# Holding back the splits of the down weights from the eighth instead of the sixteenth step of the last gate-and-up chunk

## The chip, the cores and the metric

The kernel runs on one core of one Trainium2 chip. The metric is the device time of one execution in microseconds; the median over the runs shown is compared. A core has five engines with an instruction queue each, which work in the order of the program: TensorE (PE, with its weight loads PEld), VectorE (DVE), ScalarE (ACT), GpSimd (POOL) and SyncE (SP), which here only issues loads and stores. Queues wait for each other through semaphores.

## The reference

One decoder layer on 256 tokens of width 1024, in float32: a mixer (causal pooling beside block attention), a cross-attention into 256 memory tokens, and a SwiGLU feed-forward network of width 2816. Each is followed by a residual sum, scaled by 2^0.25, and a layer norm. The change lies in the last part:

```
h = layer_norm(DEEPNORM_ALPHA * h + swiglu(h, w_gate, w_up, w_down), ln3_g, ln3_b)

def swiglu(h, w_gate, w_up, w_down):
    return (silu(h @ w_gate) * (h @ w_up)) @ w_down
```

## The kernel before

**Float32 by parts.** A float32 operand is split into a rounded high part and the low rest; a product is then three matmuls, high by high, high by low and low by high (`three`, lines 386 to 388; in gate and up the first two are one matmul of 512 columns, line 401, and the third is line 407). The activations are split once. Every weight tile (128 x 1024 numbers, 512 KB) is loaded into a raw tile, cast to its high part by ScalarE, and the low part is subtracted by VectorE (line 173).

**The stream of weights.** All weight tiles are numbered in the order of their use in one `Stream`, `ws`. There are seven raw tiles (`RAW_BUFS`), and eight buffers for split tiles and one more late in the kernel, so `ahead` is nine. `prepare` emits the split of the next tiles, and afterwards `fetch_ahead` emits loads until seven raw tiles are out and not yet split. `next`, called when a tile has been used, and `get`, called when one is wanted, prepare at most one further tile, up to nine past those used, unless `ws.held` is set; then `next` does nothing and `get` prepares only the tile that it needs itself. Where a split is emitted sets its place in the queues of ScalarE and VectorE.

**Gate and up.** The 2816 columns are worked in 11 chunks of 256 (`NFC`). A chunk has four weight tiles, w99 to w102 in the last one, and four PSUM banks, two for gate and two for up. `proj_both` yields 16 steps per chunk. In the last three chunks they go in groups of four: two steps with high parts, two with low parts; each fourth step has used up one weight tile and calls `next`. After the chunk, `Gated.add` sums the banks into SBUF (ScalarE copies at line 987, VectorE adds at line 988). `multiply` (lines 992, 993) and `split` (lines 453, 454, and 1004 to 1007 where sums are needed) follow inside the next chunk, after its second and its fourth step, and for the last chunk inside the down projection.

**Down.** Each chunk of 256 gated columns meets two tiles of w_down. Eight of the eleven chunks are multiplied as 2 x 2 blocks with seven products instead of eight, summed into eight PSUM banks m0 to m7. Four of them (`seven`, w103 to w114) build the sums of weights on VectorE and ScalarE in `prepare_pair` (lines 134 to 147): a pair is loaded as two tiles and prepared in three steps, which give three split tiles, the third, w105 for the first pair, from sums alone. The other four (`summed`, w115 to w128) load sums that transfers have made before. The last three chunks (`LAST`, w129 to w134) are multiplied plainly in `pieces`, which reads their tiles four times in all for different output columns. m1, m2, m3 and m5 take the banks of one pool, m7, m6, m4 and m0, in this order, those of the other, in which the last chunk of gate and up was summed. The first two splits of a pair are thus those around the change: w109 is the first and w110 the second of the third pair.

Behind the down products VectorE makes eight sums of m tiles and the residual (lines 1129 to 1145), adds what `pieces` yields (line 1132), takes the statistics (line 741), and the last norm follows. The end of the second half of the tokens goes through two float32 matmul pairs (lines 1180 and 1181), the second with a diagonal of the norm's scale that ScalarE makes (line 1178).

The lines around the change, with the steps counted:

```
run(gu, 2)                     # steps 1 and 2
if left: left.multiply()
run(gu, 2)                     # steps 3 and 4
if left: left.split()
if c == NFC - 1:
    run(gu, 2 * KD - 5)        # 11 more, to step 15
    ws.held = True
run(gu)                        # what is left
left = Gated(c, pss)
left.add()
# behind the loop:
ws.held = False
ws.next()
```

Of the kernel before, what the change touches and what calls it, by code (L numbers as in the profile page):

```python
# [18 lines left out]
KD = D // P  # L19
# [31 lines left out]
class Stream:  # L51
# [125 lines left out]
    def next(self):  # L177

        if not self.held:
            self.prepare(min(self.used + self.ahead, len(self.tiles) + 1))  # L180
# [27 lines left out]
def decoder_layer(  # L208
# [145 lines left out]
    def add_quarters():  # L354
        def add(dst, src):
            nc.gpsimd.dma_start(dst, src, accum_op=OP.add, max_dma_last_dim=8192)

        add(sum_z, w_sum[:, 2:4])
        add(sum_w, sum_z[:, 1:2].to_broadcast(list(sum_w.shape)))
        add(sum_w[:, 0], w_sum[:, 1])  # L360
# [32 lines left out]
    def proj_both(pss, numbers, yT, group=KD):  # L393

        for k0 in range(0, KD, group):
            for k in range(k0, k0 + group):
                hi, _ = ws.get(numbers, k)
                for b, ps in enumerate(pss):  # L400
                    nc.tensor.matmul(ps, hi[:, b * P:(b + 1) * P], yT.both(k), start=k == 0, stop=False,  # L401
                                     skip_group_check=True)
                yield
            for k in range(k0, k0 + group):
                _, lo = ws.parts_of(numbers, k)
                for b, ps in enumerate(pss):
                    nc.tensor.matmul(ps[:, S:], lo[:, b * P:(b + 1) * P], yT.pair(k)[0], start=False,  # L407
                                     stop=k == KD - 1, skip_group_check=True)
                ws.done(numbers, k)
                if ws.pace == 1:  # L410
                    ws.next()
                yield
# [31 lines left out]
    def run(gen, n=None):  # L444

        while n is None or n > 0:
            if next(gen, gen) is gen:
                return False
            n = None if n is None else n - 1
        return True  # L450
# [516 lines left out]
    def gated_t():  # L967
        pt = bank("pgt").rearrange("p (f t) -> p f t", f=2)
        for t in range(T):
            for f in range(2):  # L970
                nc.tensor.transpose(pt[:, f, t * P:(t + 1) * P], sg0[:, t, f * P:(f + 1) * P], ident)
        gated_parts(0)
        split(gT[0][0], gT[0][1], pt.rearrange("p f (t s) -> p (f t) s", t=T))
# [47 lines left out]
    for c in range(1, NFC):  # L1021
        pss = [(accbank if c % 2 else bank)("pg") for _ in range(4)]
        if c == 3:
            ws.widen(late)
            add_quarters()
        gu = proj_both(pss, c_gu[c], h2T, KD if c < NFC - 3 else 2)
        run(gu, 2)
        if left:
            left.multiply()
        run(gu, 2)  # L1030
        if left:
            left.split()
        else:
            run(gu, 4)
            gated_t()
        if c == NFC - 1:
            run(gu, 2 * KD - 5)
            ws.held = True
        run(gu)
        left = Gated(c, pss)  # L1040
        left.add()
# [199 lines left out]
```

## Time and profile before

| | |
|---|---|
| median of 3 runs | 382.67 us (382.51 to 382.80) |
| the profiled execution | 382.99 us |
| its span, first to last instruction | 381.2 us |
| mean granted TensorE clock | 0.988 |
| TensorE busy | 370.6 us, 97% of the span |
| VectorE, ScalarE busy | 303.7 us, 207.5 us |

All times within the kernel are microseconds from the start of the span of the profiled execution. A row of a timeline reads: start, duration, engine, line and operation, output and inputs, count, and in brackets the idle time before it and what ended that. A row of waits reads: who, at which line, waited for whom; microseconds in total, how often, the longest. A row of windows reads: the stretch, its length, busy time of TensorE, its weight loads, VectorE, ScalarE and GpSimd (with counts), the granted TensorE clock, the share of the DMA engines that was busy, and GB/s. Durations overlap a little with the next instruction, so a distance between two starts (a pitch) is shorter than a duration.

### The profile page before, as it was taken

The page shows a single profiled execution, that of the slowest core. Times are in us where ns is not written, and L with a number is a line of the kernel's source. Part 1 is how long each engine was busy: PE and PEld are TensorE (multiplying, and loading weights), DVE is VectorE, ACT ScalarE, POOL GpSimd, SP SyncE. Part 2 cuts the span into 40 slices and gives each one's busy share as a digit, 9 for nine tenths or more (in the row PEclk, how much of TensorE's full clock was granted, in tenths as well). Part 3 has the DMA queues.
Part 4 walks back from the last instruction along what each step waited for, and adds up shares of the span by engine and source line. Part 5 has one row for each costly group of instructions (what it writes and reads, how often), then busy time and mean ns, then how long its engine had stood idle before and what let it go on. Part 6 is the DMA issues. An engine that isn't in the chain of part 4 may idle for free.

```text
span 381.2 us, 5607 instructions
## 1 busy us (share of the span) xinstructions
PE 370.6 (97%) x2058; PEld 318.7 (84%) x2058; DVE 303.7 (80%) x490; ACT 207.5 (54%) x331; POOL 22.8 (6%) x30
## 2 busy tenths in 40 slices
PE   9999999999999999999999999999999995999994
PEld 8997878788888898988888888888898884888883
DVE  6868899965699758865887858888888899986974
ACT  5756677643164736544165666655675556766410
POOL 1000034300110000000111000000000000000021
PEclk9999999999999999999999999999999996999998
DMA  7996675578309953877179999766554134499202
GB/s 263 415 415 259 222 276 160 179 235 288 133 16 342 353 172 112 301 268 265 50 138 331 258 350 322 310 222 220 193 198 163 57 110 166 130 357 412 96 0 110
DMA packets 24268, 84.51 MB, mean 222 GB/s; under 512 B 2481, under 2 KB 3249, under 8 KB 23217
## 3 DMA queue, kind: packets, MB, share of 16 engines
q1 hardware_dynamic: 23120, 78.46, 56.7%
q0 software_dynamic: 688, 5.24, 6.7%
q10 hardware_dynamic: 432, 0.46, 0.3%
q8 instruction: 16, 0.26, 0.3%
q14 instruction: 12, 0.09, 0.1%
HBM read 83.10 MB, written 10.49 MB: 246 GB/s over the span
## 4 chain that ended last, share of the span: by engine, by line
PE 89%; DVE 6%; issue 2%; ACT 1%; DMA 1%; POOLq 0%; ACTq 0%; DVEq 0%
PE pg L401 15%; PE pg L407 8%; PE pqk L507 6%; PE m L386 5%; PE m L387 5%; PE m L388 5%; PE acc L386 4%; PE acc L387 4%; PE acc L388 4%; PE pxq L401 4%; PE pxk L401 4%; PE pxq L407 2%; PE pu L401 2%; PE pxk L407 2%; PE xv L386 2%; PE xv L388 2%
## 5 line engine op out<-in xcount | busy, mean ns | idle before, releaser
L453 ACT CAST g<-sg 128x512 fp32r<-128x512 f32 x16 | 9.9, 619 | 21.0 <-DVE sg L1007 15.1
L749 POOL TENSOR_TENSOR rs<-rs,mhalf 128x1 f32<-128x1 f32 x6 | 5.0, 832 | 264.0 <-DVE rs L748 264.0
L454 DVE TENSOR_TENSOR g<-sg,g 128x512 fp32r<-128x512 f32 x16 | 11.1, 692 | 9.6 <-ACT g L453 9.6
L988 DVE TENSOR_TENSOR sg<-pg,sg 128x256 f32<-128x256 f32 x40 | 14.1, 416 | 0.0
L992 ACT ACTIVATE sg<-sg 128x512 f32<-128x512 f32 x10 | 6.3, 632 | 14.3 <-DVE sg L988 14.3
L987 ACT COPY sg<-pg 128x256 f32<-128x256 f32 x40 | 11.8, 377 | 0.0
L544 ACT ACTIVATE xpr<-xs,mx 128x256 f32<-128x256 f32 x8 | 3.7, 470 | 14.3 <-DVE mx L555 14.3
L544 ACT ACTIVATE pr<-pr,mx 128x128 f32<-128x128 f32 (+1 forms) x16 | 7.1, 445 | 7.6 <-DVE mx L575 7.6
L453 ACT CAST h2T<-tp 128x512 fp32r<-128x512 f32 x4 | 2.3, 586 | 12.9 <-PE tp L464 12.9
L754 DVE SCALAR_TENSOR_TENSOR r<-r,mv,gb 128x512 f32<-128x512 f32 (+2 forms) x12 | 8.3, 723 | 0.0
L741 DVE BATCH_NORM_STATS2 st<-r 128x6 f32<-128x512 f32 (+1 forms) x12 | 8.0, 670 | 0.3
L993 DVE TENSOR_TENSOR sg<-sg 128x512 f32<-128x512 f32 x10 | 6.9, 692 | 0.8
L620 POOL TENSOR_TENSOR win<-upad 128x542 f32<-128x542 f32 x2 | 4.0, 2000 | 57.0 <-DVE upad L651 57.0
L549 DVE RECIPROCAL sm<-sm 128x2 f32<-128x2 f32 x12 | 2.0, 166 | 6.0 <-ACT xpr L544 4.5
L859 PE MATMUL xs<-xkTh,xq 128*128 128x256 f32 x32 | 6.4, 282 | 0.0
L453 ACT CAST h1T<-tp 128x512 fp32r<-128x512 f32 x4 | 2.4, 588 | 7.1 <-PE tp L464 7.1
L759 DVE SCALAR_TENSOR_TENSOR h<-r,rs,gb 128x512 f32<-128x512 f32 x8 | 5.7, 747 | 0.1
L620 POOL TENSOR_TENSOR win<-win 128x269 f32<-128x269 f32 (+3 forms) x4 | 5.8, 1444 | 0.2
L659 ACT CAST xkTh<-pxk 128x256 fp32r<-128x256 f32 x8 | 2.6, 377 | 5.5 <-PE pxk L407 5.5
L661 DVE TENSOR_TENSOR xkl<-pxk,xkTh 128x256 f32<-128x256 f32 x8 | 3.0, 415 | 3.1 <-ACT xkTh L659 3.1
L859 PEld LDWEIGHTS xs<-xkTh,xq 128*128 128x128 f32 x32 | 5.2, 190 | 0.2
L171 ACT CAST w39h<-w39r 128x1024 fp32r<-128x1024 f32 x1 | 1.0, 1049 | 7.8 <-PE acc L388 7.8
(1148 smaller groups left out, 1295.1 us busy)
## 6 DMA issues: line engine op xcount, KB each, us to landing
sum_z<-in_w_sum SPq DMA_DIRECT2D x1, 2048.0 KB, 10.4
sum_w<-in_w_sum SPq DMA_DIRECT2D x1, 2048.0 KB, 10.4
sum_z<-in_w_sum POOLq DMA_DIRECT2D x1, 2048.0 KB, 13.9
sum_w<-sum_z POOLq DMA_DIRECT2D x1, 2048.0 KB, 17.9
gb<-in_ln_g SPq DMA_DIRECT2D x3, 512.0 KB, 6.6
gb<-in_ln_b SPq DMA_DIRECT2D x3, 512.0 KB, 8.9
wr<-in_w_qkv SPq DMA_DIRECT2D x5, 256.0 KB, 4.5
mr<-in_mem_t SPq DMA_DIRECT2D x1, 1024.0 KB, 11.1
```

What stands on the lines that cost most here:

```text
L386: nc.tensor.matmul(ps, wa, ya, start=start, stop=False, skip_group_check=part)
L387: nc.tensor.matmul(ps, wa, yb, start=False, stop=False, skip_group_check=part)
L388: nc.tensor.matmul(ps, wb, ya, start=False, stop=stop, skip_group_check=part)
L401: nc.tensor.matmul(ps, hi[:, b * P:(b + 1) * P], yT.both(k), start=k == 0, stop=False, skip_group_check=True)
L407: nc.tensor.matmul(ps[:, S:], lo[:, b * P:(b + 1) * P], yT.pair(k)[0], start=False, stop=k == KD - 1, skip_group_check=True)
L453: nc.scalar.copy(h, ps)
L454: nc.vector.tensor_sub(l, ps, r32(h))
L507: nc.tensor.matmul(qk[i][:, f, :], w[:, c * P:(c + 1) * P], y, start=k == 0 and f == 0 and w is hi and y is x_hi, stop=k == KD - 1 and w i ...
L544: nc.scalar.activation(dst[:, j, :], src[:, j, :], AF.Exp, bias=mx[:, j:j + 1], scale=sign, accum_out=sm[:, j:j + 1])
L859: nc.tensor.matmul(ps[:, t, :], q[:, kk, t * P:(t + 1) * P], k[:, 2 * h + kk], start=n == 0, stop=q is q_lo and kk == 1, skip_group_check= ...
L987: nc.scalar.copy(y[:, f, :], ps[:, S:])
L988: nc.vector.tensor_add(y[:, f, :], ps[:, :S], y[:, f, :])
```

## The change

In the last chunk (c = 10) the hold is set after 3 more steps instead of 11, so after 7 of the 16 steps instead of 15. The preparation that steps 8 and 12 would emit is then left out there, as that of step 16 was already. The hold ends where it did, behind `left.add()`; the tiles are prepared from there on, one at each call of `next`.

```
         if c == NFC - 1:
-            run(gu, 2 * KD - 5)
+            run(gu, 3)
             ws.held = True
         run(gu)
         left = Gated(c, pss)
```

More of the change, by code (lines that the diff above doesn't have):

```diff
@@ L1036, in decoder_layer @@
         if c == NFC - 1:
-            run(gu, 2 * KD - 5)
+            run(gu, 3)
             ws.held = True
```

## The prediction

> **What bounds the kernel now.** I read the page first, then TensorE's waits, then the timeline of each engine from 310 us to the end, then VectorE's and the loads' rows for the down projection. The page says that TensorE is the bound almost everywhere, with one hole near the end.
>
> ```profile
> PE 370.6 (97%) x2058; PEld 318.7 (84%) x2058; DVE 303.7 (80%) x490; ACT 207.5 (54%) x331; POOL 22.8 (6%) x30
> PE   9999999999999999999999999999999995999994
> PEclk9999999999999999999999999999999996999998
> ```
>
> The 5 of the busy tenths and the 6 of the clock stand in slice 34 (each slice is 9.53 us, so about 314.5 to 324). The waits of TensorE name it, and a timeline of TensorE shows its size:
>
> ```profile
> PE m L386 <- DVE sg L988: 4.1, 1, 4.1
> 314.93 0.39 PE L388 MATMUL m<-w104h,g 128*128 128x512 f32 x1
> 319.38 0.80 PE L386 MATMUL m<-w104h,g 128*128 128x512 f32 x1 [4.07 <-DVE sg L988]
> 319.98 0.63 PE L387 MATMUL m<-w104l,g 128*128 128x512 f32 x1
> 328.70 0.39 PE L386 MATMUL m<-w109c,g 128*128 128x512 f32 x1
> 333.46 0.39 PE L386 MATMUL m<-w112c,g 128*128 128x512 f32 x1
> 317.00:318.00 1.00, 0.00 (x0) 0.00 (x0) 1.00 (x3) 0.22 (x2) 0.00 (x0) 0.81 0.00 0
> ```
>
> The fifth product of the down projection writes m7, whose PSUM bank is the first of the four in which the last chunk of gate and up was summed. That bank is free only when VectorE's first add (line 988) has read it. VectorE is busy the whole time; this is what it does meanwhile:
>
> ```profile
> 313.63 0.69 DVE L136 TENSOR_TENSOR w111r<-w109r 128x512 f32<-128x512 f32 x1
> 317.17 0.69 DVE L143 TENSOR_TENSOR w109r<-w110r,w109r 128x512 f32<-128x512 f32 x1
> 317.78 1.22 DVE L144 TENSOR_TENSOR w110l<-w111r,w110h 128x1024 fp32r<-128x1024 f32 x1
> 318.91 1.41 DVE L988 TENSOR_TENSOR sg<-pg,sg 128x256 f32<-128x256 f32 x4
> 320.24 1.22 DVE L147 TENSOR_TENSOR w111l<-w109r,w111h 128x1024 fp32r<-128x1024 f32 x1
> 321.37 0.69 DVE L993 TENSOR_TENSOR sg<-sg 128x512 f32<-128x512 f32 x1
> 322.74 0.69 DVE L454 TENSOR_TENSOR go<-sg,go 128x512 fp32r<-128x512 f32 x1 [0.69 <-ACT go L453]
> 323.35 0.69 DVE L136 TENSOR_TENSOR w114r<-w112r 128x512 f32<-128x512 f32 x1
> 326.90 0.68 DVE L143 TENSOR_TENSOR w112r<-w113r,w112r 128x512 f32<-128x512 f32 x1
> 327.50 1.22 DVE L144 TENSOR_TENSOR w113l<-w114r,w113h 128x1024 fp32r<-128x1024 f32 x1
> ```
>
> From 313.63 to 318.91 it splits w109 and w110, which TensorE reads only at 328.70 and later, while the adds that TensorE needs wait behind them in VectorE's order.
>
> **What the change moves.** In the last chunk the two splits that were emitted at its 8th and 12th step, w109 and w110, are held, so they come after the adds. Moved are seven instructions of VectorE (lines 136 to 140, 143, 144: 318.91 - 313.63 = 5.28 us) and three casts of ScalarE. These two calls of `prepare` issue no loads: with three pairs or their parts unsplit, `fetch_ahead` already has seven raw tiles out at w115, and it goes on only when w111 is split. The order of SP's loads is thus unchanged; POOL issues nothing here. Nothing is added or removed.
>
> **Term 1, TensorE at the seam.** VectorE comes to the adds at 313.63; TensorE has then finished the gate and up sums (its first eleven products of down are issued by 314.93), and ScalarE, without the three casts, is free for its copies. The first add takes 1.41/4, about 0.4 us: m7 is free at 314.05. TensorE would want it one pitch after its row at 314.93; 21 matmuls from 328.70 to 333.46 give a pitch of 0.227, so at 315.16. The wait is gone: 319.38 - 315.16 = 4.22 us. With it goes the half clock that the hole leaves behind (0.63 us for a matmul against 0.39): from 319.38 to 328.70 there are 30 matmuls in 9.32 us, and at the full pitch they take 6.80, so another 2.52. From w109 on TensorE could be 6.74 us earlier.
>
> **Term 2, the splits that come later.** After the adds the program's order on VectorE is w109, multiply (993), split of the gated tile (454), w110, w111, then w112. The same instructions as before lie between 313.63 and w112's first, so it starts at 323.35 again, plus one bubble: w111's cast on ScalarE waits for line 143 and VectorE then has only line 144 to fill with.
>
> ```profile
> 317.95 1.05 ACT L146 CAST w111h<-w109r 128x1024 fp32r<-128x1024 f32 x1 [0.78 <-DVE w109r L143]
> 335.73 0.39 PE L387 MATMUL m<-w113l,g 128*128 128x512 f32 x1
> ```
>
> The cast starts 0.78 us after line 143 does and takes 1.05; VectorE is free 0.61 + 1.13 after it; with a hand-over the bubble is 0.12. So w112 and all behind it come 0.12 later than before, while TensorE reads them 6.74 earlier. w109 (ready at 313.63 + 1.33 for the adds + 3.54 + the tail of its last instruction, 318.6) is wanted at 321.96. The tightest is w113's low part: ready at 327.50 + 1.22 + 0.12 = 328.84, wanted at 335.73 - 6.74 = 328.99. That cover is 0.15 us thick; if it is gone TensorE waits by what VectorE is late, and by term 3 up to 1 us of that costs nothing. The lead falls from nine tiles to seven, as `next` prepares one per tile used.
>
> **Term 3, the loads.** This is where the gain ends. The last tiles are bound by transfers:
>
> ```profile
> SPq L103 <- DVE w112r L143: 8.2, 1, 8.2
> 327.65 0.38 SPq L103 DMA_DIRECT2D w119r<-in_w_sum  x1
> 323.00:328.00 5.00, 5.00 (x20) 4.07 (x19) 5.00 (x8) 2.54 (x4) 0.00 (x0) 0.85 0.03 11
> 335.00:355.00 20.00, 20.00 (x90) 16.53 (x90) 15.26 (x13) 13.51 (x13) 0.00 (x0) 1.00 1.02 391
> 349.01 1.05 ACT L171 CAST w129h<-w129r 128x1024 fp32r<-128x1024 f32 x1 [1.44 <-DMA w129r<-in_w_down]
> 351.52 1.05 ACT L171 CAST w130h<-w130r 128x1024 fp32r<-128x1024 f32 x1 [1.46 <-DMA w130r<-in_w_down]
> 356.61 1.05 ACT L171 CAST w134h<-w134r 128x1024 fp32r<-128x1024 f32 x1 [0.20 <-DMA w134r<-in_w_down]
> 357.49 0.39 PE L387 MATMUL m<-w129l,go 128*128 128x512 f32 x1
> 358.85 0.39 PE L387 MATMUL m<-w130l,go 128*128 128x512 f32 x1
> ```
>
> SP waits 8.2 us for line 143 of w112 before it issues w119; the engines of the DMA idle (a share of 0.03 from 323 to 328), and from 335 to 355 they are full (1.02). So the stream of w119 to w134 starts when w112's line 143 ends and then runs at the rate of the transfers. Line 143 stays at 326.90 plus 0.12, so w134 lands where it did, plus 0.12. (w117 and w118, released by w109's line 143 and w110's 144, go out 3.3 us later, since 317.17 becomes about 320.5; they fall into the idle stretch.) TensorE, early by 6.74, wants w129's low part at 350.75 and w130's at 352.11 or later. Cast and subtraction end 1.09 + 1.23 us after a cast starts (as at 356.61 and 357.70, next fence), so they are ready at 351.45 and 353.96: TensorE waits 0.7, then about 1.2 more, and is early by 358.85 - 353.96 = 4.9 us from there on.
>
> **Term 4, VectorE's tail.** Behind w134's subtraction VectorE has eight sums of 0.6 us, then norm 3.
>
> ```profile
> 357.70 1.22 DVE L173 TENSOR_TENSOR w134l<-w134r,w134h 128x1024 fp32r<-128x1024 f32 x1
> 358.84 0.68 DVE L1129 SCALAR_TENSOR_TENSOR r<-h,m 128x512 f32<-128x512 f32 x1
> 364.94 1.37 DVE L1132 TENSOR_TENSOR r<-m,r 128x512 f32<-128x512 f32 x2 [1.22 <-PE m L388]
> 369.70 0.69 DVE L1132 TENSOR_TENSOR r<-m,r 128x512 f32<-128x512 f32 x1 [0.24 <-PE m L388]
> 371.85 0.42 DVE L1132 TENSOR_TENSOR r<-m,r 128x256 f32<-128x256 f32 x1 [0.73 <-PE m L388]
> 374.23 0.43 DVE L741 BATCH_NORM_STATS2 st<-acc 128x6 f32<-128x256 f32 x1 [1.49 <-PE acc L388]
> ```
>
> VectorE's waits for TensorE from here to the end are 1.22 + 0.24 + 0.73 + 1.49 = 3.68 us. With TensorE early by 4.9 all of them go; overlap with the next instruction (0.08 at each of the four places, 0.69 of duration against a pitch of 0.61) gives back another 0.3. VectorE then carries the end by itself. The later chain (mean, power on POOL, ScalarE's diagonal, two matmuls, copy, store) hangs on the last statistics and moves with them.
>
> **The sum.** 3.68 + 0.32 - 0.12 = 3.9 us. Against its own time, 382.99 for a span of 381.2, the profiled execution would be 379.1; the median shown, 382.67, lies 0.3 below that execution, which makes 378.8. The bounds: all of TensorE's 6.74 if nothing behind holds it back (375.9), and from the other side the whole 5.28 us of moved work landing on the release of w119 (3.9 - 5.3 = -1.4, so 384.1). I take the value near the first end, since VectorE's rows show no place where the moved work meets a wait.
>
> **Rivals.** *The half clock at the end.* TensorE would finish its last products and the first of its two final pairs 4.9 us earlier, but the last pair waits for the diagonal, only 3.9 earlier.
>
> ```profile
> 374.03 0.81 PE L1180 MATMUL end<-gb,ident 128*128 128x384 f32 x2
> 376.31 0.91 PE L1181 MATMUL end<-r,diag 128*128 128x384 f32 x2 [1.46 <-ACT diag L1178]
> 314.20:317.60 3.40, 1.12 (x5) 0.57 (x4) 3.40 (x6) 2.14 (x5) 0.00 (x0) 1.00 0.47 154
> ```
>
> The idle time of 1.46 becomes about 2.4. At the seam the clock fell 2.3 us after TensorE stopped (0.81 in the second from 317 means full speed until 317.62), at the end of a stretch in which it was still busy for 1.12 of 3.40 us. If it falls so again, the last pair takes 0.91 x 0.63/0.39 or more, so 0.6 to 0.9 longer, on the path: 379.6. [...]
>
> *The loads are not the bound.* If w119's stream came earlier with TensorE, up to 6.7 us would be gained: 376.0. Against it stand the full transfers from 335 to 355 and casts that wait for them to the end.
>
> *Slower: the release of w119 slips.* The held splits keep the raw tiles of w109 to w111 longer. If VectorE came to w112's line 143 not 0.12 but the whole 5.28 us later, because it had to wait after the adds for what the moved splits used to cover, the stream of loads and the end would move with it: 384.0. It decides from a slip of 4.0 us on, as the end depends on it one to one. For it: the stream has no slack. Against: only the waits of 0.69 and 0.12 stand in VectorE's new order.
>
> *Nothing much happens.* Another wait at the seam takes the place of this one (ScalarE's copies, or the down tiles starving TensorE from w112 on): 382.6. Against: m7's first reader is the only wait of TensorE there, and a starved TensorE costs nothing for its first microsecond.
>
> **How the numbers follow.** Forecast 0.60 (its own range 378.0 to 379.3), half clock 0.20, loads not the bound 0.07, slower 0.08, nothing much 0.05. About 0.2% is what a measurement of this kernel tells from no change. The range of 377.2 to 380.3 leaves out the three small cases, 0.2 in all. Faster: 0.60 + 0.20 + 0.07 and half of the last, 0.89; same 0.03; slower 0.08.
>
> **What would show it.** Right: no wait of TensorE at line 386 for line 988, no half clock near 320; line 988 at about 313.6, ahead of w109; w119 issued at 327.7 to 327.8; TensorE waiting about 1 us at w129 and w130; VectorE's subtraction of w134 at about 357.8; its waits for TensorE at line 1132 gone. Wrong: w119 issued over 1 us later or earlier, waits of TensorE at w112 to w118, or w134's cast elsewhere than 356.7.

## The result, and the profile after

The changed kernel takes 379.09 us (median of 6, 378.74 to 379.92); the kernel before, on the same chip, 382.74 (382.40 to 383.57). The ratio is 0.9906 with a 95% interval of 0.9892 to 0.9920: faster by 3.6 us, between 3.1 and 4.1. The forecast was 378.8.

The page of the kernel after (busy time of TensorE, its 40 slices and its granted clock) no longer has the hole in slice 34:

```profile
PE 369.6 (98%) x2058; PEld 317.6 (84%) x2058; DVE 303.0 (80%) x490; ACT 207.1 (55%) x331; POOL 22.7 (6%) x30
PE   9999999999999999999999999999999999999993
PEclk9999999999999999999999999999999999999998
```

The waits of TensorE after show no line 988; what is left near the end is one wait at w130, and a longer one for the diagonal:

```profile
PE end L1181 <- ACT diag L1178: 2.1, 1, 2.1
...
PE m L387 <- DVE w130l L173: 0.8, 1, 0.8
```

The timeline of TensorE after has the fifth product of down, the one that waited, in step with its neighbours, and w112 six microseconds earlier than before (327.27 against 333.46):

```profile
315.48 0.39 PE L388 MATMUL m<-w104h,g 128*128 128x512 f32 x1
315.71 0.39 PE L386 MATMUL m<-w104h,g 128*128 128x512 f32 x1
327.27 0.39 PE L386 MATMUL m<-w112c,g 128*128 128x512 f32 x1
354.49 0.50 PE L387 MATMUL m<-w130l,go 128*128 128x512 f32 x1 [0.76 <-DVE w130l L173]
```

The timelines of VectorE after: the adds (988) stand right behind the gated split (454), and w109 (line 136) behind the adds. At the tail line 1132 and the statistics of acc have no idle time in brackets any more.

```profile
313.87 0.69 DVE L454 TENSOR_TENSOR go<-sg,go 128x512 fp32r<-128x512 f32 x1
314.48 1.41 DVE L988 TENSOR_TENSOR sg<-pg,sg 128x256 f32<-128x256 f32 x4
315.80 0.68 DVE L136 TENSOR_TENSOR w111r<-w109r 128x512 f32<-128x512 f32 x1
324.39 0.69 DVE L136 TENSOR_TENSOR w114r<-w112r 128x512 f32<-128x512 f32 x1
327.94 0.68 DVE L143 TENSOR_TENSOR w112r<-w113r,w112r 128x512 f32<-128x512 f32 x1
358.31 1.22 DVE L173 TENSOR_TENSOR w134l<-w134r,w134h 128x1024 fp32r<-128x1024 f32 x1
364.25 1.28 DVE L1132 TENSOR_TENSOR r<-m,r 128x512 f32<-128x512 f32 x2
370.71 0.41 DVE L741 BATCH_NORM_STATS2 st<-acc 128x6 f32<-128x256 f32 x1
```

The loads after (issue of w119, the cast of w130, and the DMA engines' share in windows of 318 to 324 and 335 to 355 us):

```profile
328.69 0.38 SPq L103 DMA_DIRECT2D w119r<-in_w_sum  x1
352.13 1.05 ACT L171 CAST w130h<-w130r 128x1024 fp32r<-128x1024 f32 x1 [1.78 <-DMA w130r<-in_w_down]
318.00:324.00 6.00, 6.00 (x28) 4.99 (x27) 5.31 (x7) 3.52 (x5) 0.00 (x0) 1.00 0.07 27
335.00:355.00 20.00, 19.09 (x83) 15.17 (x82) 15.62 (x14) 12.91 (x13) 0.00 (x0) 1.00 1.01 388
```

One thing must be known to compare the two traces. The programs are the same up to the seam, but the profiled execution after came there 0.84 us later: the gated split that starts at 313.87 after starts at 313.03 before.

```profile
313.03 0.68 DVE L454 TENSOR_TENSOR go<-sg,go 128x512 fp32r<-128x512 f32 x1
```

Counted from that instruction to the end of the span, the kernel took 381.2 - 313.03 = 68.17 before and 377.6 - 313.87 = 63.73 after, 4.4 less; 0.84 of it was lost ahead of the seam, and 3.6 is left for this pair of executions. The lag differs between executions of all kernels here (the same split starts between 312.76 and 313.97 in those whose last chunk is unchanged up to it); its cause was not looked for. Below, traces are compared from such common points. Less the lag, w119 was issued at 327.85 and w134's subtraction started at 357.47, where 327.7 to 327.8 and about 357.8 were named.

### The profile page after: what moved, and what is told of

Same layout as the page of the kernel before. It is cut to its first block, busy times and chain, and to the rows that moved or that the text cites. A ratio compares the mean times of both kernels' runs of the same rounds, so it can differ in the third digit from the quotient of the medians.

```text
span 377.6 us, 5603 instructions
## 1 busy us (share of the span) xinstructions
PE 369.6 (98%) x2058; PEld 317.6 (84%) x2058; DVE 303.0 (80%) x490; ACT 207.1 (55%) x331; POOL 22.7 (6%) x30
## 4 chain that ended last, share of the span: by engine, by line
PE 76%; DVE 12%; DMA 4%; ACT 3%; issue 2%; POOL 1%; POOLq 0%; ACTq 0%; DVEq 0%
PE pg L401 15%; PE pg L407 8%; PE pqk L507 6%; PE pxk L401 4%; PE pxq L401 4%; PE acc L386 4%; PE acc L387 4%; PE acc L388 4%; DMA w134r<-in_w_down 2%; PE pxq L407 2%; PE pu L401 2%; PE pxk L407 2%; DMA w127r<-sum_z 2%; PE xv L386 2%; PE xv L388 2%
```

## The experiments

Ratios are to the kernel before, run on the same chip. "VectorE at w112" is line 143 of w112, which releases w119, and "at w134" its last subtraction.

**Hold after 11 steps.** On the kernel after:

```
-            run(gu, 3)
+            run(gu, 7)
             ws.held = True
```

> The hold starts after 11 of the 16 steps, so w109 is split ahead of the adds of line 988 and w110 behind them. Theory (the splits ahead of the adds are the stall, and loads plus VectorE's tail cap what its removal brings): the first add comes 3.5 us later than in the changed kernel and 1.7 earlier than in the one before; TensorE waits about 2.4 us at line 386 instead of 4.1. If the clock still falls in that hole the time is about 380.7 (2.0 under the kernel before), if it does not, TensorE is early by up to 4.3 and the cap of 3.6 applies: 379.1. Rival (the stall depends on something else in the last chunk, not on how much is split ahead): a wait of 4.1 as before and 382.7, or none at all.

380.13 us, ratio 0.9927 (0.9911 to 0.9943). The rows are a wait of TensorE, the adds, and a window of the clock:

```profile
PE m L386 <- DVE sg L988: 2.5, 1, 2.5
318.05 1.41 DVE L988 TENSOR_TENSOR sg<-pg,sg 128x256 f32<-128x256 f32 x4
318.00:324.00 6.00, 5.48 (x24) 4.55 (x25) 5.06 (x10) 2.80 (x5) 0.00 (x0) 1.00 0.35 105
```

The adds are 3.57 us later than after the change, as foreseen (w109 lies between), and the wait is 2.5 where 2.4 was worked out: the stall is the splits ahead of the adds. The clock stayed at 1.00. The profiled execution took 379.74 us against 379.43 of the one after: the 2.5 us of waiting cost at most 0.3, which fits the cap, and that much is the release, since line 143 of w112 came 328.24 - 313.90 = 14.34 after the gated split instead of 14.07. The median does not fit the cap as well: by the ratios it is 0.8 above the change (0.9927 against 0.9906). The mean clocks of the four executions are 0.996, 0.995, 0.992 and 0.997, and the slowest, 380.56, is the one at 0.992; a fall of the clock may explain that one, but two of the others, 380.09 and 380.17, stay unexplained.

**No hold at all.** On the kernel before:

```
         if c == NFC - 1:
-            run(gu, 2 * KD - 5)
-            ws.held = True
+            run(gu)
```

> The kernel before without any hold in the last chunk: w109, w110 and w111 are all split ahead of the adds. Theory: the first add comes 1.1 us later than before, TensorE waits 5.2 us instead of 4.1 and has the half clock behind it, and its end, which sets the time there, moves with it: 383.9. Rival (the wait at the seam is covered by slack elsewhere): 382.9 as before.

384.55 us, ratio 1.0043 (1.0030 to 1.0055), so 1.6 slower. TensorE's wait, its last matmul before it, and the clock's window:

```profile
PE m L386 <- DVE sg L988: 5.7, 1, 5.7
315.24 0.39 PE L388 MATMUL m<-w104h,g 128*128 128x512 f32 x1
319.00:320.00 1.00, 0.00 (x0) 0.00 (x0) 0.95 (x2) 1.00 (x3) 0.00 (x0) 0.81 0.09 8
```

The wait for line 988 is 1.6 longer, not 1.1, and the time follows it. The direction and the place are as foreseen, the size somewhat larger: counted from the gated split (at 313.70 here) the adds (at 320.87) start after 7.17 instead of 5.88, 1.3 later, and TensorE came to its wait 0.3 earlier. With three, two, one and none of the splits ahead of the adds the wait is 5.7, 4.1, 2.5 and 0.

**Hold for the whole last chunk.** On the kernel after:

```
+        ws.held = c == NFC - 1
         run(gu, 2)
...
             run(gu, 3)
-            ws.held = True
```

> The changed kernel with the hold set from the first step of the last chunk, so that w108 too is split behind the adds. Theory: TensorE has no wait at the seam left to win, VectorE does the same work ahead of w112's line 143, and w108 is ready before TensorE reads it: 379.1 as the changed kernel, within 0.4. Rival (every split held back from the adds brings some 1.1 us): 378.0.

379.78 us, ratio 0.9911 (0.9888 to 0.9934): the same as the change. The adds start at 313.48, and with w108 behind them nothing is won. The rival, 1.1 us for each split held, falls: a hold pays only as far as TensorE waits.

**Norm loads early.** On the kernel after:

```
-    ws.before(c_dn[LAST[0]][0], load_norm("g", 3, ln3_g))
-    ws.before(c_dn[LAST[0]][1], load_norm("b", 3, ln3_b))
+    ws.before(c_dn[5]["z"], load_norm("g", 3, ln3_g))
+    ws.before(c_dn[5]["z"], load_norm("b", 3, ln3_b))
```

> The changed kernel with the two loads of norm 3's g and b issued ahead of w116, where the DMA engines idle, instead of between w128 and w130. Theory (the end is bound by the stream of loads to w134, then by VectorE): the casts of w129 to w134 come about 2.5 us earlier, TensorE no longer waits at w130, and the end moves with it, to about 376.6. Rival (TensorE's and VectorE's own work is the bound, the loads only look so): 379.1 as the changed kernel.

376.82 us, ratio 0.9841 (0.9826 to 0.9855): 6.1 under the kernel before, and by the two ratios 2.5 under the changed one (0.0065 of 383). VectorE at w112 and at w134, and the cast of w130, which waited 1.78:

```profile
327.65 0.69 DVE L143 TENSOR_TENSOR w112r<-w113r,w112r 128x512 f32<-128x512 f32 x1
349.20 1.05 ACT L171 CAST w130h<-w130r 128x1024 fp32r<-128x1024 f32 x1 [0.22 <-DMA w130r<-in_w_down]
355.60 1.23 DVE L173 TENSOR_TENSOR w134l<-w134r,w134h 128x1024 fp32r<-128x1024 f32 x1
```

From the release to w134 it is 27.95 us instead of 30.37, and TensorE's wait at w130 is gone. The loads were the bound. This kernel beats both.

**The same on the kernel before** (the same two lines moved).

> The kernel before with the same early loads of norm 3's g and b as in the run on norm loads. Theory: before the change TensorE, late by the stall, is the bound of the end and the loads have slack, so the casts of w129 to w134 come about 2.5 us earlier and nothing is gained: 382.9. Rival (the loads bound both kernels): some 2.3 us less, 380.6.

383.27 us, ratio 1.0002 (0.9989 to 1.0015): nothing. VectorE's subtraction of w134, and the first add of `pieces`:

```profile
354.55 1.23 DVE L173 TENSOR_TENSOR w134l<-w134r,w134h 128x1024 fp32r<-128x1024 f32 x1
363.69 1.37 DVE L1132 TENSOR_TENSOR r<-m,r 128x512 f32<-128x512 f32 x2 [3.11 <-PE m L388]
```

The stream is as much shorter here (326.63 to 354.55, 27.9), but VectorE then waits 3.11 us for TensorE instead of 1.22. This profiled execution, 381.72, was the fastest of ten, so the verdict rests on the medians (383.27 against 383.16). The bound is TensorE before the change and the stream of loads after it.

**The last gated tile late.** On the kernel after:

```
-    run(dn, 2)
+    run(dn, 35)
     left.multiply()
```

> The changed kernel with the last chunk's multiply and split (lines 993 and 454, read by TensorE only at w133) moved behind the splits of about w124, so that VectorE comes to w112 about 2.0 us earlier. Theory (w112's line 143 releases w119 and starts the stream that sets the end): w119 is issued 2.0 us earlier, w134 is cast 2.0 earlier, the time is about 377.1. Rival (the stream has a start or a rate of its own): w134's cast does not move, 379.1.

377.34 us, ratio 0.9849 (0.9830 to 0.9868): 5.8 under the kernel before, 377.1 expected. The issue of w119 and of w132, SP's wait before the latter, VectorE at w112 and at w134, and the last pair of TensorE:

```profile
326.44 0.38 SPq L103 DMA_DIRECT2D w119r<-in_w_sum  x1
345.37 0.33 SPq L103 DMA_DIRECT2D w132r<-in_w_down  x1
SPq L103 <- DVE w125l L173: 3.1, 1, 3.1
325.68 0.69 DVE L143 TENSOR_TENSOR w112r<-w113r,w112r 128x512 f32<-128x512 f32 x1
356.75 1.23 DVE L173 TENSOR_TENSOR w134l<-w134r,w134h 128x1024 fp32r<-128x1024 f32 x1
371.23 1.62 PE L1181 MATMUL end<-r,diag 128*128 128x384 f32 x2 [2.13 <-ACT diag L1178]
```

Line 143 of w112 comes 2.26 us earlier than after the change, 0.33 of it an earlier seam (the gated split at 313.54), so 1.9 as foreseen. From there to w134 it took 0.7 longer (31.07), so w134 comes 1.56 earlier, or 1.2 without the seam. The longer stretch comes at least in part from the edit itself: the moved gated work now stands between the splits of w124 and w125, and the load of w132, which takes w125's raw tile, is issued 3.46 us after that of w131 (at 341.91) instead of 1.29 as after the change. This profiled execution, at 378.12, was the slowest of the four; its last pair, of 1.62 us against 0.91, is taken up below. By the ratios the gain of the medians on the changed kernel is 2.2.

**The release made late.** On the kernel after, three sums whose result nothing reads, before w112 is split:

```
+    def late_release():
+        for _ in range(3):
+            nc.vector.tensor_add(waste, h2[:, 0, :512], h2[:, 0, 512:])
...
+    ws.before_split(c_dn[4][0], late_release)
```

> The changed kernel with three sums of 128x512 of no use on VectorE (1.8 us at a pitch of 0.60) between w111 and w112. Theory (the end depends one to one on the release of w119): w119 issued 1.8 us later, w134 cast 1.8 later, 380.9. Rival (only TensorE's waits for splits count): TensorE waits some 1.5 us more at w113, has about 1 us of that to spare, and the time is 379.1 to 379.6.

381.09 us, ratio 0.9956 (0.9942 to 0.9970), 380.9 expected. VectorE at w112 and w134, and TensorE's waits:

```profile
329.88 0.68 DVE L143 TENSOR_TENSOR w112r<-w113r,w112r 128x512 f32<-128x512 f32 x1
361.00 1.23 DVE L173 TENSOR_TENSOR w134l<-w134r,w134h 128x1024 fp32r<-128x1024 f32 x1 [0.71 <-ACT w134h L171]
...
PE m L387 <- DVE w112l L140: 0.8, 1, 0.8
...
PE m L387 <- DVE w130l L173: 0.8, 1, 0.8
```

1.94 us later at w112 gives 1.9 us in the medians (by the ratios, 0.9956 against 0.9906). The profiled execution, 382.14, was the slowest of six, and w134 came 2.69 later in it. TensorE does starve at w112, and still stands waiting at w130 as without the sums: these waits are absorbed, the release is not.

**Both: norm loads early, gated tile late.**

> The changed kernel with both: norm loads early and the last gated tile late. Theory: the stream of loads would end 4.5 us earlier, but TensorE's own work is the bound from some 6.7 us under the kernel before; norm loads alone already reach 6.2, so only about 0.3 more: 376.5. Rival (the loads bound still): 374.9.

377.03 us, ratio 0.9844 (0.9822 to 0.9866), the same as norm loads alone, where 0.3 less was expected. The subtraction of w134, TensorE's one wait for a split, and the statistics of acc, which have an idle time for TensorE again:

```profile
355.49 1.21 DVE L173 TENSOR_TENSOR w134l<-w134r,w134h 128x1024 fp32r<-128x1024 f32 x1
346.54 0.50 PE L387 MATMUL m<-w125l,g 128*128 128x512 f32 x1 [0.46 <-DVE w125l L173]
368.88 0.43 DVE L741 BATCH_NORM_STATS2 st<-acc 128x6 f32<-128x256 f32 x1 [0.92 <-PE acc L388]
```

VectorE waits 0.92 us for TensorE at the end, so TensorE ends last again. Whether a shorter stream would bring something isn't shown, because the stream is hardly shorter here: from the gated split (at 313.97) to w134 it took 41.52 us, with the norm loads alone 355.60 - 313.58 = 42.02. The moved gated work holds up w125, SP waits 3.1 us for it as with the gated tile alone, and TensorE loses 0.5 us at w125.

**Busy at the end, and the change once more.** In the first, on the kernel after:

```
+    keep_busy(7)
     nc.tensor.matmul(ps, diag, norm.r[:, CUT:], start=False, stop=True)
```

> The changed kernel with seven products of zeros between the two final matmul pairs, in the hole in which TensorE waits for the diagonal. Theory (the half clock at the end falls in some executions of the changed kernel and not in others, 0.4 to 0.7 us longer where it does): no half clock at the last pair, the times no longer spread upwards, and the median some 0.3 under the unaltered changed kernel of the same chip: about 378.8. Rival (the clock at the last pair is not on the path, or the zeros delay it): the same or up to 0.5 more.

> The changed kernel as it is, for a profile of a second execution and times beside the kernel with the busy end: 379.1. Theory (the half clock at the end comes and goes): the last pair takes between 0.9 and 1.6 us in this execution as well, and a slower one goes with a longer time.

379.14 us (378.42 to 379.63) and 379.20 (378.99 to 379.37), ratios 0.9901 and 0.9903. The last pair, busy and not:

```profile
372.29 0.91 PE L1182 MATMUL end<-r,diag 128*128 128x384 f32 x2 [0.56 <-ACT diag L1178]
```

```profile
372.27 0.91 PE L1181 MATMUL end<-r,diag 128*128 128x384 f32 x2 [2.10 <-ACT diag L1178]
```

The granted clock was 1.00 during the last pair in both profiled executions (in the microseconds from 372 and from 373), the spread is no smaller, and the medians lie 0.06 apart: the half clock at the end isn't seen in the changed kernel's median. With four runs each and intervals of about 0.6 to either side, the 0.3 that was expected could not be told from nothing.

## Why the prediction was right

**Term 1, the seam.** TensorE no longer waits at line 386 for line 988: the adds follow the gated split after 0.61 us, and w112 is reached 327.27 - 313.87 = 13.40 us after that split instead of 20.43, so 7.0 earlier where 6.7 was worked out. The four placings of the hold show that the wait grows with each split ahead of the adds.

**Term 2, the later splits.** VectorE came to w112 10.52 us after the gated split, 10.32 before: 0.20 later, forecast 0.12. The cover at w113, worked out at 0.15 us, was gone: TensorE reads w113's low part 0.48 after the matmul before, against a pitch of 0.23, so it waited 0.25, which the list of waits doesn't show. As foreseen, this cost nothing.

```profile
329.34 0.40 PE L386 MATMUL m<-w113h,g 128*128 128x512 f32 x1
329.82 0.50 PE L387 MATMUL m<-w113l,g 128*128 128x512 f32 x1
```

**Term 3, the loads.** Here the gain was to end, and it did. Release and end moved together, late and early (all of these but the last with the norm loads where they were):

| kernel | line 143 of w112 | w134's subtraction | between |
|---|---|---|---|
| before | 326.90 | 357.70 | 30.80 |
| after | 327.94 | 358.31 | 30.37 |
| after, once more | 327.49 | 357.79 | 30.30 |
| no hold | 327.91 | 359.65 | 31.74 |
| gated tile late | 325.68 | 356.75 | 31.07 |
| release late | 329.88 | 361.00 | 31.12 |
| norm loads early | 327.65 | 355.60 | 27.95 |

The forecast took the stretch as fixed; it lies between 30.0 (busy at the end) and 31.7 in the kernels with the norm loads in place. One to one is thus what the medians show, not each trace. Part of the difference may hang on TensorE: in the kernel before, the casts of w123 to w127 waited for TensorE, 0.26 to 1.06 us each, after the change for transfers, 0.24 to 0.76. No run tests this alone. The row is of w123 in the kernel before:

```profile
339.85 1.05 ACT L171 CAST w123h<-w123r 128x1024 fp32r<-128x1024 f32 x1 [1.06 <-PE m L388]
```

TensorE's waits were forecast at 0.7 for w129 and 1.2 for w130. At w129 there was none: the cast of w129 came 20.61 us after the issue of w119 instead of 21.36 before, so the low part was ready at 351.61, and TensorE read it at 351.73. At w130 it lost 1.3 us, 0.30 at its first matmul and 1.03 at its second over the pitch of 0.23; the list shows 0.8 of that.

```profile
350.38 1.23 DVE L173 TENSOR_TENSOR w129l<-w129r,w129h 128x1024 fp32r<-128x1024 f32 x1 [1.27 <-ACT w129h L171]
351.73 0.43 PE L387 MATMUL m<-w129l,go 128*128 128x512 f32 x1
352.70 0.39 PE L388 MATMUL m<-w129h,go 128*128 128x512 f32 x1
353.23 0.50 PE L386 MATMUL m<-w130h,go 128*128 128x512 f32 x1
```

**Term 4, VectorE's tail.** From w134's subtraction to the end it was 381.2 - 357.70 = 23.50 before and 377.6 - 358.31 = 19.29 after: 4.2 gained, 4.0 worked out (3.68 + 0.32). The four waits for TensorE are gone.

**The sum.** From the seam: 4.21 in the tail, 0.43 in the stream, less 0.20, which is the 4.4 of the traces. The 3.9 forecast is 0.5 under that and lies within the interval of the medians (3.1 to 4.1). That it came so near is in part luck, because the sum was worked out on an execution that lost more than most. The kernel before has two levels of the mean clock: of its 34 executions beside the experiments 11 are at 0.988 or 0.989 and take 383.3 us on average, 23 at 0.991 to 0.993 and take 382.8. The profiled one, at 0.988, is of the first kind, with the half clock from 317.62 to 324.44. In the profiled execution with the norm loads early on the kernel before, at 0.991, it lasted from 318.72 to 322.12 only, and from the gated split to the end it was 379.9 - 312.76 = 67.14 instead of 68.17. Measured against these two, the gain from the seam on is 4.4 and 3.4.

**The rivals.** *Loads not the bound* falls by the norm loads, which bring 2.5 us here and nothing on the kernel before. *Slower by a slip of the release*: the mechanism exists and goes about one to one in the medians, as the late release shows (1.94 us at w112, 1.9 in the medians), but the slip was 0.2 and not 5.3. *Nothing much*: no other wait took the place. *Half clock at the end*: the hole came as forecast, 2.1 us against the 2.4 foreseen, but in both profiled executions of the changed kernel the last pair kept its 0.91, at a granted clock of 1.00. It did lengthen in three others, with holes of 2.13, 2.48 and 2.12 us: 1.62 with the gated tile late, 1.33 with the release late, 1.51 with the hold over the whole chunk, each with a granted clock of 0.50 in the microsecond in which the pair ended. So it comes and goes, and the last pair takes 0.4 to 0.7 longer where it comes.

## What to carry to other kernels

What is prepared ahead stands in the queue ahead of what is urgent, as here 5.28 us of splits ahead of the adds: where an engine lags behind the one that it feeds, hold back preparation whose reader is far away until the result that frees the reader's next buffer is through. The worth of a removed stall is not its length but the distance to what is late next; here a TensorE that was 7.0 us earlier at the seam brought 3.6, because a stream of loads, started by a buffer's release, came next. Moving two loads out of that stream was worth nothing before and 2.5 us after, so look for the next bound again once a stall is gone.

## What the runs showed of the hardware

The clock of TensorE did not fall at a fixed idle time. The mean clock in a window of one microsecond (1.00 until the fall, 0.50 from it) gives the moment: 2.3 us after the last matmul in the kernel before, 4.0 without a hold (0.81 in the microsecond from 319, with TensorE idle from 315.63), 3.5 with the norm loads early on the kernel before, and not at all in a hole of 2.53 us with the hold after 11 steps. Worked out in the same way, the half clock lasted 6.8 us in the kernel before and 3.4 with the norm loads early on it. Without a hold the matmuls tell where it ended: they take 0.63 us up to the one at 325.77, 0.52 at 326.20 and 0.39 from 326.55 on, so it lasted from 319.62 to about 326.4, an estimated 6.8 us. The first two rows are of the kernel before, the other two of that with its norm loads early:

```profile
318.00:319.00 1.00, 0.00 (x0) 0.00 (x0) 1.00 (x2) 0.99 (x1) 0.00 (x0) 0.50 0.00 0
324.00:325.00 1.00, 1.00 (x5) 0.82 (x4) 1.00 (x3) 0.45 (x2) 0.00 (x0) 0.78 0.00 0
318.00:319.00 1.00, 0.00 (x0) 0.00 (x0) 1.00 (x3) 0.72 (x1) 0.00 (x0) 0.86 0.00 0
322.00:323.00 1.00, 1.00 (x6) 0.83 (x5) 0.52 (x1) 1.00 (x3) 0.00 (x0) 0.94 0.63 258
```

What sets the moment of the fall and the length of the half clock, no run here shows.
